# A hybrid attention and SSD layer: V by seven-product jobs, and split operands of x rebuilt on chip at each change of token half

## The chip, the cores and the metric

The kernel runs on one core of a Trainium2 chip. The metric is the device time of one execution in microseconds (us); the time before is the median of three runs. A profile of one further execution is shown beside it. Engines are called by their names in the profile: PE is TensorE (matmuls; PEld its weight loads), DVE is VectorE, ACT is ScalarE, POOL is GpSimd, SP is SyncE, which only issues DMAs. A lower-case q behind an engine's name is its sequencer.

## The reference, cut to what matters

One decoder layer for 2048 tokens of width 1024 in float32. All that the change touches is the input projection `x @ w_in` (1024 x 6672) and, in it, the columns of V and the 16 raw time steps of the SSM.

```python
proj = jnp.einsum('bsd,de->bse', x, w_in[layer])
q, k, v, z_att, z_ssm, xbc, dt_raw = jnp.split(proj, list(SPLITS), axis=-1)
# q, k, v, z_att, z_ssm: 1024 columns each; xbc: 1536; dt_raw: 16
...
o1, l1 = dilated_window_attention(q, k, v, slopes, DILATIONS[0])   # and two more dilations
...
xbc = jax.nn.silu(causal_depthwise_conv(xbc, conv_w[layer], conv_b[layer]))
dt = jax.nn.softplus(dt_raw.astype(jnp.float32) + dt_bias[layer].astype(jnp.float32))
...
y = ssd_chunked(xs_h, dt, a, bm, cm)                                # Mamba-2 scan
...
out = jnp.einsum('bse,ed->bsd', mix, w_out[layer])
x = layer_norm(alpha * x + out, ln_g[layer], ln_b[layer])
```

## The kernel before, in words

**Precision.** A float32 product is made of three fast matmuls. Each operand is split into a high part (ScalarE copies it to the fast type, `nc.scalar.copy`) and a low part (the difference, by VectorE for tokens and by GpSimd for weights), and high x high, low x high and high x low are added up in PSUM.

**The V stage** (lines 90 to 160, driven by the loop over `order` from line 647 on). It comes first. All 1040 columns of V and the time steps are made in plain products with the tokens as stationary operand: for two token halves, three pieces of 348, 346 and 346 columns, eight slices of the contraction and eight groups of 128 tokens, three matmuls each (`v_mm`, L151; 1152 in all). Beside it the stage loads x, splits it (`conv_x`, L140 and L141) and makes and stores what the later jobs need: the split operands of the second token half go to a DRAM tensor `d_T` (`keep_second`), those of the first stay on chip (`T0`) and are stored too (`keep_T`). It also splits half of `w_out`.

**The seven-product jobs.** The other 6144 columns are made 256 columns x 1024 tokens at a time, as a 2 x 2 block product with seven instead of eight block products (Winograd's form of Strassen's method). The token operands of the seven are, in order, `LEFT = ("B11", "T1", "B21", "T2", "B22", "T4", "T3")` with T1 = B12 - B11, T2 = B22 - T1, T3 = B22 - B12, T4 = T2 - B21; each is [128, 4, 512] and has a high and a low part, 16 KB a partition together. The weight operands are A11, S1 = A21 + A22, A12, and so on, made by `column_side` (L288 the sums on VectorE, L295 the high part on ScalarE, L296 the low part on GpSimd). `products` issues 12 matmuls of 512 columns for each of the seven (L340, L342, L344), copies the partial results p1, p5, u2 and p4 out of PSUM on ScalarE (`keep`, L349) into a pool of six buffers `ev`, adds the others to them on VectorE (`put`, L357), and hands each finished block to a `fin`, which stores it a step later. After each product `flush()` runs what was put down for that step with `after(n, f)`; so a job has seven steps, and the side work of the next job (weights, loads) is put down step by step by hand. PE, DVE, ACT and POOL execute in the order in which the program is written (`manual_schedule`); SP's queue is ordered by the scheduler.

**Phases.** Ten jobs work on the first token half, then 22 on the second (their changed weight operands are stored in `d_wc` for reuse), then 12 on the first half again with the weights read back (`column_reload`). At each of the two changes `token_side` reads all seven split operands of the other half, 14 MB, from `d_T` through GpSimd's DMA queue, each as soon as the last job has used the old one. During jobs 1 to 4 the differences T1 to T4 of the second half are made and stored (`sums_load`, `sums_part`, L199 to L203). The time-step arithmetic of the SSM (`decays`, L484 to L520) is spread over steps 12 to 33, and the SSD units (`ssd1` to `ssd5`) run between the products from step 164 on. `copy_v` makes a second copy of V in DRAM in another order of tokens.

**After the projections** come attention for eight pairs of heads (L895 to L978) and the output product with the norm (L1131 to L1169), which the change doesn't touch; attention loads V from `d_v` (L834, L836).

Of the kernel before, what the change touches and what calls it, by code (L numbers as in the profile page):

```python
# [28 lines left out]
def hybrid_layer(ctx, tc, xT, xc, w52, wv, convw, convb, dtb, alog, dskp, gcol, wout,  # L29
# [12 lines left out]
    def dtile(name, shape):  # L42
# [10 lines left out]
    d_T = {(p, n): dtile(f"d_T{p}{n}", [2, 128, 4, 512]) for p in range(2)  # L53
           for n in ("B11", "B21", "B22", "T1", "T2", "T3", "T4")}
# [15 lines left out]
    def evac(i, o, a):  # L70
        if i % 2:
            nc.vector.tensor_copy(o, a)
        else:
            nc.scalar.copy(o, a)

    LEFT = ("B11", "T1", "B21", "T2", "B22", "T4", "T3")
    with ExitStack() as c1:
        pp = c1.enter_context(tc.tile_pool(name="pp", bufs=5, space=PSUM))
        ss = c1.enter_context(tc.tile_pool(name="ss", bufs=3, space=PSUM))

        tp = c1.enter_context(tc.tile_pool(name="tp", bufs=1, reuse_waits="tile"))

        def operand(nm):
            return [tp.tile([128, 4, 512], F32R, name=f"T{nm}{x}") for x in "hl"]  # L90

        def keep_T(nm, a):
            nc.scalar.dma_start(d_T[0, nm][a].rearrange("p k t -> p (k t)"),
                              T0[nm][a].bitcast(F32).rearrange("p k t -> p (k t)"))

        vstage, early = ExitStack(), ExitStack()
        ts = early.enter_context(tc.tile_pool(name="ts", bufs=1, reuse_waits="tile"))
        vp = vstage.enter_context(tc.tile_pool(name="vp", bufs=1, side="right", reuse_waits="tile"))
        T0 = {nm: operand(nm) for nm in ("B11", "B21", "B22")}
        B12 = [vp.tile([128, 4, 512], F32R, name=f"B12{x}") for x in "hl"]  # L100
        second = [operand(f"T{c}") for c in range(1, 5)]

        def x_op(k, i, a):

            if i:
                return second[k // 2][a][:, 2 * (k % 2):2 * (k % 2) + 2]
            left, right = (T0["B11"], B12) if k < 4 else (T0["B21"], T0["B22"])
            return left[a][:, k % 4], right[a][:, k % 4]

        COLS = ((0, 348), (348, 346), (694, 346))  # L110
        vw, vr, rows = {}, {}, {}

        def ask_v(pc, k, queue=nc.gpsimd):
            c0, w = COLS[pc]
            vr[k] = vp.tile([128, 348], F32, name="vraw", bufs=3)[:, 0:w]
            queue.dma_start(vr[k], wv[:, k, c0:c0 + w])
# [1279 lines left out]
```

## Time and profile before

| | |
|---|---|
| median of three runs | 2073.09 us (2069.44 to 2076.03) |
| the profiled execution | 2074.26 us, of it span 2072.5 us |
| PE busy | 1979.0 us, 95% of the span |
| DVE, ACT, POOL busy | 60%, 54%, 52% |
| DMA moved | 481.51 MB, mean 232 GB/s |
| first matmul of the V stage | 6.16 us after the span's start |
| V stage, first to last matmul | 6.16 to 192.7 us |
| seven-product jobs | 192.7 to 1196.9 us |
| attention and output | from there to the end |

A busy PE row counts the pipelined length of each matmul, so the distance between the starts of two matmuls says more than the mean length of one. In the waits, the arrow names what ended an engine's idle time. A row of stretches has one window of time, and in brackets the instructions that lie in it or reach into it.

### The profile page before, as it was taken

What the parts mean: (1) busy time and instruction counts of PE and PEld (TensorE: products, weight loads), DVE (VectorE), ACT (ScalarE), POOL (GpSimd) and SP (SyncE); (2) the same over time, 40 slices, a digit from 0 to 9 for tenths busy, and PEclk for the clock granted to TensorE, in tenths of its full rate; (3) what the DMA queues carried; (4) which work ended last, traced back from release to release, by engine and by line L of the source; (5) the groups of instructions that cost most, each with busy time, mean ns of one, the idle gap of its engine ahead of it and who ended that gap; (6) DMA issues with size and microseconds to landing.
All of it is one profiled execution on the core that took longest, in us unless ns stands there. A gap on an engine that the chain in (4) does not pass through costs nothing.

```text
span 2072.5 us, 42407 instructions
## 1 busy us (share of the span) xinstructions
PE 1979.0 (95%) x15744; PEld 1616.2 (78%) x15744; DVE 1236.8 (60%) x3166; ACT 1125.8 (54%) x3097; POOL 1079.0 (52%) x966
## 2 busy tenths in 40 slices
PE   8999899889999999979999999999899988999998
PEld 8999778778888888858888867667666766888886
DVE  2353666357886656624444368777777846565553
ACT  3433455346655666536566478888778852232221
POOL 4445346656665666735555423687666572422222
PEclk9999999999999999989999999999999999999999
DMA  9797897967678887897878755787877799232210
GB/s 313 268 307 236 267 318 277 368 226 223 202 231 292 276 259 252 321 362 230 275 245 254 250 203 155 223 242 220 239 223 219 230 271 321 96 114 98 89 69 31
DMA packets 238238, 481.51 MB, mean 232 GB/s; under 512 B 38448, under 2 KB 110896, under 8 KB 225872
## 3 DMA queue, kind: packets, MB, share of 16 engines
q1 hardware_dynamic: 147648, 199.52, 30.7%
q0 software_dynamic: 45024, 181.49, 25.9%
q10 hardware_dynamic: 45360, 97.80, 14.9%
q8 instruction: 124, 2.03, 0.4%
q14 instruction: 82, 0.67, 0.1%
HBM read 323.15 MB, written 163.97 MB: 235 GB/s over the span
## 4 chain that ended last, share of the span: by engine, by line
PE 77%; DMA 10%; DVE 5%; ACT 3%; issue 3%; POOL 1%; SPq 1%; ACTq 0%; POOLq 0%; DVEq 0%
PE pp L340 11%; PE pp L344 11%; PE pp L342 11%; PE pp L151 6%; PE N L948 5%; PE S L895 4%; PE S L1131 4%; PE S L1133 3%; PE S L1132 3%; PE ss L151 3%; PE T L922 3%; ACT P L907 2%; PE T L1131 2%; PE T L1132 2%; PE T L1133 2%
## 5 line engine op out<-in xcount | busy, mean ns | idle before, releaser
L296 POOL TENSOR_TENSOR w<-wr,w 128x512 fp32r<-128x512 f32 x231 | 306.1, 1335 | 223.1 <-ACT w L295 173.8
L907 ACT ACTIVATE P<-P,st 128x192 f32<-128x192 f32 (+1 forms) x768 | 322.7, 423 | 72.3 <-DVE st L901 67.4
L901 DVE CUSTOM_DVE_ANT_0 P<-S,tb 128x192 f32<-128x192 f32 (+1 forms) x768 | 206.6, 325 | 98.5 <-PE S L895 80.8
L349 ACT COPY ev<-pp 128x512 f32<-128x512 f32 x176 | 103.0, 585 | 251.7 <-PE pp L344 236.9
L357 DVE TENSOR_TENSOR ev<-pp,ev 128x512 f32<-128x512 f32 x152 | 101.1, 686 | 138.6 <-PE pp L344 95.0
L295 ACT CAST w<-wr 128x512 fp32r<-128x512 f32 x231 | 140.1, 620 | 56.2 <-DVE wr L288 40.0
L1039 POOL TENSOR_TENSOR wb<-num,wb 128x2048 f32<-128x2048 f32 x21 | 95.6, 4551 | 117.4 <-DMA wb<-d_wd 55.1
L907 ACT ACTIVATION_READ_ACCUMULATOR P<-P,st 128x1 f32 x768 | 145.6, 190 | 0.0
L288 DVE TENSOR_TENSOR wr<-wr 128x512 f32<-128x512 f32 x132 | 122.1, 925 | 30.9 <-DMA wr<-w 26.9
L948 PE MATMUL N<-PT,v 128*64 128x64 f32 (+1 forms) x1536 | 126.1, 261 | 12.6 <-ACT num L972 9.0
L924 DVE COPY PT<-T 128x512 f32<-128x512 f32 x192 | 131.8, 686 | 4.6 <-PE T L922 4.6
L922 PE MATMUL T<-ident,P 128*128 128x128 f32 x768 | 129.5, 292 | 1.3 <-DVE st L901 0.9
L922 PEld LDWEIGHTS T<-ident,P 128*128 128x128 f32 x768 | 82.7, 143 | 48.6 <-issue 24.3
L948 PEld LDWEIGHTS N<-PT,v 128*64 128x64 f32 x1536 | 78.8, 138 | 50.6 <-issue 18.9
L895 PE MATMUL S<-k,ex 64*64 64x192 f32 (+1 forms) x2048 | 111.7, 329 | 5.2 <-issue 5.2
L441 DVE SCALAR_TENSOR_TENSOR ss<-U,cw,ss 128x512 f32<-128x512 f32 x144 | 106.0, 751 | 3.7 <-ACT ss L437 1.4
L122 POOL TENSOR_TENSOR vl<-vraw,vh 128x346 fp32r<-128x346 f32 (+1 forms) x48 | 49.1, 1023 | 91.0 <-ACT vh L121 90.8
L1169 POOL TENSOR_TENSOR k<-k,wb 128x1024 f32<-128x1024 f32 x8 | 25.8, 3226 | 121.9 <-DVE k L1168 121.9
L1107 DVE TENSOR_REDUCE tb<-P 128x128 f32<-128x1024 f32 x30 | 60.0, 1999 | 44.9 <-ACT P L1104 22.6
L895 PEld LDWEIGHTS S<-k,ex 64*64 64x64 f32 x2048 | 67.5, 137 | 18.0 <-issue 11.8
L574 DVE TENSOR_TENSOR mt<-mt,ss 128x1024 f32<-128x1024 f32 x32 | 39.0, 1220 | 69.4 <-ACT mt L570 69.0
L565 ACT ACTIVATE mt<-csb,cs 128x128 f32<-128x128 f32 x256 | 78.7, 395 | 3.2 <-DMA csb<-d_cs 2.3
(542 smaller groups left out, 6074.6 us busy)
## 6 DMA issues: line engine op xcount, KB each, us to landing
wr<-w ACTq DMA_DIRECT2D x157, 256.0 KB
wb<-d_wd SPq DMA_DIRECT2D x48, 512.0 KB
d_wc<-w SPq DMA_DIRECT2D x44, 512.0 KB
w<-d_wc POOLq DMA_DIRECT2D x44, 512.0 KB, 6.2
csb<-d_cs ACTq DMA_DIRECT2D x32, 512.0 KB
v<-d_v POOLq DMA_DIRECT2D x16, 1024.0 KB, 6.8
vs<-d_v POOLq DMA_DIRECT2D x16, 960.0 KB, 8.6
st<-xT POOLq DMA_DIRECT2D x20, 512.0 KB, 6.2
```

The source lines that it names most:

```text
L151: nc.tensor.matmul(ps, l if j == 2 else h, vw[k][j % 2], start=(k == j == 0), stop=(k == 7 and j == 2))
L295: nc.scalar.copy(t[:, 0], q[nm])
L296: nc.gpsimd.tensor_tensor(t[:, 1], q[nm], t[:, 0].bitcast(F32), op=OP.subtract)
L340: nc.tensor.matmul(ps, w[:, 0, k], th[:, k], start=start and k == 0, stop=False, skip_group_check=not start)
L342: nc.tensor.matmul(ps, w[:, 0, k], tl[:, k], start=False, stop=False, skip_group_check=not start)
L344: nc.tensor.matmul(ps, w[:, 1, k], th[:, k], start=False, stop=(k == 3), skip_group_check=not start)
L895: nc.tensor.matmul(o, A["q"][d][64 * h:64 * h + 64, blk, 64 * a:64 * a + 64], kv, start=True, stop=True)
L901: nc.vector.tensor_tensor_reduce(P[:, h, cs], sp[h][:, cs], t, -0.125, 3.0e38, OP.add, OP.min, accum_out=stat(A, 0, d, h, blk))
L907: nc.scalar.activation(p, p, AF.Exp, bias=stat(A, 0, d, h, blk), scale=-1.0, accum_out=stat(A, 1, d, h, blk))
L922: nc.tensor.transpose(tp[:, h, i], P[:, h, 256 * i:256 * i + 128], ident)
L924: nc.vector.tensor_copy(pt, tp)
L948: nc.tensor.matmul(o, l, r, start=start, stop=True, skip_group_check=True)
```

## The change

V becomes four wide seven-product jobs of 512 columns x 1024 tokens: V's first half of columns opens phase 0 and phase 1, its second half is the second job of phase 1 and the first of phase 2. In a wide job the tokens are the stationary operand (128 x 128) and 256 weight columns stream; each of the seven products is 16 x 3 matmuls into two PSUM banks (`wide_products`). The weight operands of a wide job are made on chip at its first use, stored (`d_wv`, 1 MB an operand) and read back at its second (`wide_reload`).

The separate V stage, `d_T` and everything that filled it are gone. At the start and at each change of token half, a class `Tokens` loads the four raw blocks of x (1 MB each, `xb`) into places that the old operands have left, and makes the seven split operands from them on VectorE and ScalarE (`STEPS`), put down at steps 3 to 11 counted from the start of the last job of the old half.

The 16 time-step columns leave V's pieces: `steps_of` makes them for each token half during a wide job, with the weights as stationary operand (32 columns: high and low side by side, then 16) and 512 tokens streaming, 32 matmuls a half, and turns the result by twelve small transposes. All 32 half rows of `w_out` are split in steps 8 to 60 (before: half of it in the V stage). `decays` moves into the third wide job. `copy_v` copies V by halves of columns, the second half in phase 2. The pool of weight operands `wp` holds pairs of narrow operands in the tiles of wide ones. There are now 48 jobs (0 to 47) of seven steps; 0, 11, 12 and 35 are the wide ones.

```diff
-        def v_mm(ps, pc, i, r, k, which=(0, 1, 2)):
...
-        def token_side(p):
-
-            T = []
-
-            def step(nm):
-                def f():
-                    T.append([tp.tile([128, 4, 512], F32R, name=f"T{nm}{x}") for x in "hl"])
-                    for a, t in enumerate(T[-1]):
-                        nc.gpsimd.dma_start(t.rearrange("p k t -> p (k t)"),
-                                            d_T[p, nm][a].rearrange("p k t -> p (k t)"))
-                return f
-            return T, [step(nm) for nm in LEFT]
...
+        class Tokens:
...
+            def load(self, n, queue, cuts=1):
+                src = xb[self.p, (0, 1, 3, 2)[n]]
+                if n == 0:
+                    self.r["X"] = x = [wp.tile([128, 512], F32, name="wr", bufs=7) for _ in range(4)]
+                    for k in range(4):
+                        queue.dma_start(x[k], src[:, 512 * k:512 * k + 512])
+                    return
+                nm, at, y = (("R12", "B21", "l"), ("R22", "T4", "l"), ("R21", "T4", "h"))[n - 1]
+                t = self.r[nm] = home(at, y, F32)
...
+            def split(self, nm, src, ks):
+                if ks[0] == 0:
+                    T[nm] = [home(nm, x) for x in "hl"]
+                for s in self.cut(ks, (src,)):
+                    h, l, r = T[nm][0][:, s], T[nm][1][:, s], self.at(src, s)
...
+                    nc.scalar.copy(h, r)
+                    nc.vector.tensor_tensor(l, r, h.bitcast(F32), op=OP.subtract)
...
+            STEPS = (("split", "B11", "X"), ("minus", "X", "R12", "X"), ("split", "T1", "X"),
+                     ("minus", "T2", "R22", "X", ("B22", "l")), ("minus", "X", "R22", "R12"), ("split", "B21", "R21"),
+                     ("minus", "T4", "T2", "R21", ("T3", "l")), ("split", "T2", "T2"), ("split", "B22", "R22"),
+                     ("split", "T4", "T4"), ("split", "T3", "X"))
...
+        def wide_reload(W, s):
+
+            def step(i):
+                nc.gpsimd.dma_start(W[i].rearrange("p a k c -> p (a k c)"), d_wv[s, i])
+            return [lambda i=i: step(i) for i in range(7)]
...
+        def wide_products(W, fin, ramp=False):
+
+            def mm(ps, i, start=True):
+                w, (th, tl) = W[i], T[LEFT[i]]
+                order = [(r, k) for r in range(4) for k in range(4)]
+                if ramp and i < 4:
+                    order.sort(key=lambda x: x[1])
+                for r, k in order:
+                    o, t = ps[r // 2][:, 256 * (r % 2):256 * (r % 2) + 256], slice(r * NJ, r * NJ + NJ)
+                    for j in range(3):
+                        nc.tensor.matmul(o, (th, tl)[j == 1][:, k, t], w[:, int(j == 2), k],
+                                         start=start and r % 2 == k == j == 0, stop=(k == 3 and j == 2),
+                                         skip_group_check=True)
...
+            both = lambda ps: [keep(x) for x in ps]
+            t = [pp.tile([128, 512], F32, name="pp") for _ in range(4)]
+            pa, pc = t[0::2], t[1::2]
+            mm(pa, 0)
+            p1 = both(pa)
+            flush()
+            mm(pc, 1)
+            p5 = both(pc)
+            flush()
+            pb = [ss.tile([128, 512], F32, name="ss") for _ in range(2)]
+            mm(pb, 2)
+            put(0, 0, pb, p1)
+            flush()
+            mm(pa, 3, False)
+            u2 = both(pa)
+            flush()
+            mm(pc, 4, False)
+            put(0, 1, pc, u2)
+            flush()
+            pd = [ss.tile([128, 512], F32, name="ss") for _ in range(2)]
+            mm(pd, 5)
+            p4 = both(pd)
+            flush()
+            mm(pa, 6, False)
+            put(1, 1, pa, p5)
+            put(1, 0, pa, p4, OP.subtract)
+            flush()
...
+            def sums():
+                for pair in (("B11", "B21"), ("T1", "B22")):
+                    ps = ss.tile([128, 512], F32, name="ss")
+                    for a, nm in enumerate(pair):
+                        for k in range(4):
+                            for j, w in ((0, 32), (1, 16)):
+                                nc.tensor.matmul(ps[0:w, :], wd[:, k + 4 * a, 0:w], T[nm][j][:, k],
+                                                 start=(a == k == j == 0), stop=(k == 3 and j == 1), skip_group_check=True)
+                        if a or nm == "B11":
+                            e = ev.tile([128, 512], F32, name="ev")
+                            nc.scalar.copy(e[0:32], ps[0:32])
+                            got.append(e)
...
-        jobs = [(0, x) for x in one_ + conv[4:]]
+        jobs = [(0, ("v", 0))] + [(0, x) for x in one_ + conv[4:]]
+        jobs += [(1, ("v", 0)), (1, ("v", 1))]
         jobs += [(1, x) for x in one_ + [conv[4], rest[0], conv[5]] + rest[1:]]
-        jobs += [(2, x) for x in rest]
+        jobs += [(2, ("v", 1))] + [(2, x) for x in rest]
...
-        spots = [7 * 23 + 3 + 60 * i // 13 if i < 13 else 7 * 32 + 4 * (i - 13) for i in range(32)]
+        spots = [7 * 26 + 2 + 4 * i if i < 13 else 7 * 36 + 4 * (i - 13) for i in range(32)]
...
+                    fs, times = wide_reload(W, i), (1, 3, 6, 7, 8, 9, 10)
...
+            for j in range(32):
+                later.setdefault(8 + 27 * j // 16, []).append(lambda j=j: wout_load(wo, j))
...
+                    if jobs[m + 1][0] != ph:
+                        tok = Tokens(jobs[m + 1][0] % 2)
+                        for t, n in zip((0, 3, 5, 5), range(4)):
+                            after(t, lambda n=n, k=tok: k.load(n, nc.gpsimd))
+                        for t, n in ((3, 0), (5, 1), (6, 2), (6, 3), (6, 4), (7, 5), (7, 6), (8, 7), (9, 8), (10, 9), (11, 10)):
+                            after(t, lambda n=n, k=tok: k.step(n))
```

In the start's own schedule (not shown) SP asks for the weights A11, the x block B11, R12, A21, A22, R22, A12 and R21 in this order. In a wide job `dt` (the three parts of `steps_of`) is put down at steps 3, 5 and 6 of job 0 and 1, 5 and 6 of job 11, and the parts of `decays` at steps 1 to 6 of job 12.

More of the change, by code (lines that the diff above doesn't have):

```diff
@@ L52, in hybrid_layer @@
     d_zs = [dtile(f"d_zs{g}", [16, 128, 2, 4, 64]) for g in range(2)]
[L53 to L54 removed]
+    d_wv = dtile("d_wv", [2, 7, 128, 2048])
     d_cu = [dtile(f"d_cu{i}", [128, 2, 512]) for i in range(12)]
@@ L98, in hybrid_layer @@
[L98 to L116, printed above, removed]
-        def conv_v(pc, k):
-            w, raw = COLS[pc][1], vr[k]
-            vw[k] = vh, vl = [vp.tile([128, 348], F32R, name=f"v{p}{k}")[:, 0:w] for p in "hl"]
-            nc.scalar.copy(vh, raw)
-            nc.gpsimd.tensor_tensor(vl, raw, vh.bitcast(F32), op=OP.subtract)
@@ new lines, in column_load, with load, first @@
+        def column_load(q, ct0, ct1, queue, part=False):
+            def load(nm, ct, h):
+                q[nm] = wp.tile([128, 4, 128], F32, name="wr", bufs=7)
+                queue.dma_start(q[nm], w52[ct][:, 4 * h:4 * h + 4, :])
+            def first():
+                if not part:
+                    q["S1"] = wp.tile([128, 4, 128], F32, name="wr", bufs=7)
+                load("A11", ct0, 0)
+            steps = [first, lambda: load("A12", ct0, 1), lambda: load("A22", ct1, 1)]
+            return steps if part else steps + [lambda: load("A21", ct1, 0)]
@@ new lines, in prepare @@
+        def prepare(m):
+            ph, (kind, i) = jobs[m + 1]
+            wide_now = jobs[m][1][0] == "v"
+            W, q = layout[m + 1], Q.setdefault(m + 1, {})
+            if kind == "v":
+                if ph == 1 and i == 1:
+                    two, fs = column_side(W, q, keep_wide(1))
+                    times = (4, 4, 5, 6, 6, 7, 8, 9, 10)
+                else:
+                    fs, times = wide_reload(W, i), (1, 3, 6, 7, 8, 9, 10)
+            elif ph == 2:
+                fs = column_reload(W, rest.index((kind, i)), q)
+                times = (4, 4, 5, 5, 6, 6, 7) if wide_now else (1, 2, 3, 4, 5, 7, 8)
+            else:
+                u = rest.index((kind, i)) if ph == 1 and (kind, i) in rest else None
+                two, fs = column_side(W, q, keep_sums(u))
+                times = (4, 6, 6, 6, 6, 7, 7, 8, 9) if wide_now else (1, 2 + (m == 1), 3 + (m == 1), 3, 4, 5, 6, 7, 8)
+            for t, f in zip(times, fs):
+                after(t, f)
@@ L777, in hybrid_layer @@
[L777 to L787 removed]
+                    prepare(m)
```

561 lines of the change are left out of this document (258 added, 303 removed).

## The prediction

> **What bounds the kernel now.** I read the page first, then the chain of waits, then busy time by stretches cut at the first matmul of jobs, then the waits of TensorE.
>
> ```profile
> span 2072.5 us, 42407 instructions
> PE 1979.0 (95%) x15744; PEld 1616.2 (78%) x15744; DVE 1236.8 (60%) x3166; ACT 1125.8 (54%) x3097; POOL 1079.0 (52%) x966
> ...
> PE 77%; DMA 10%; DVE 5%; ACT 3%; issue 3%; POOL 1%; SPq 1%; ACTq 0%; POOLq 0%; DVEq 0%
> ```
>
> TensorE is busy nearly always and carries 77% of the chain, so a change pays only through the matmuls' pace or through the holes between them. The stretches say where the holes are (columns: stretch, its length, then per engine the busy time with the count of instructions, last the granted clock, the DMA share and GB/s).
>
> ```profile
> core 0: us, PE busy (x) PEld busy (x) DVE busy (x) ACT busy (x) POOL busy (x), PEclk, DMA share, GB/s
> 6.16:192.70 186.54, 186.54 (x1152) 186.36 (x1153) 75.95 (x100) 71.81 (x134) 99.41 (x134) 1.00 0.87 294
> 230.80:282.10 51.30, 42.88 (x173) 34.28 (x173) 42.00 (x61) 26.11 (x44) 18.57 (x14) 0.93 0.86 298
> 377.80:396.90 19.10, 19.10 (x86) 15.80 (x85) 5.79 (x8) 6.48 (x12) 15.45 (x19) 1.00 0.98 354
> 396.90:432.40 35.50, 24.48 (x85) 17.57 (x84) 5.61 (x10) 6.22 (x12) 14.40 (x17) 0.90 0.98 378
> 879.40:923.80 44.40, 32.39 (x126) 24.57 (x126) 12.84 (x22) 18.75 (x39) 18.77 (x20) 0.81 1.05 392
> 923.80:1196.90 273.10, 273.10 (x1524) 227.33 (x1522) 122.84 (x234) 155.82 (x318) 144.88 (x149) 1.00 0.78 252
> ```
>
> Row 1 is the old V stage, 1152 matmuls without a hole. Row 3 is one undisturbed seven-product job: 84 matmuls (the count takes in two that reach over the edges) in 19.1 us, 0.227 us each at 512 columns. Rows 4 and 5 are the two jobs after a change of token half: the same 84 matmuls take 35.5 us, and 44.4 us where the eleven jobs behind, with the same SSD work among them, take 273.1 / 11 = 24.8 us. Row 2 is two jobs that should take 38.1 us. The waits say what for:
>
> ```profile
> PE pp L340 <- ACT ev L349: 9.3, 4, 5.3
> PE pp L342 <- DMA TB21l<-d_T1B: 3.3, 1, 3.3
> PE pp L342 <- DMA TB21l<-d_T0B: 3.2, 1, 3.2
> ```
>
> At the changes TensorE waits for the split operands that come back from DRAM (14 MB for one half), at 378 to 392 GB/s with the DMA engines full. In row 2 it waits for an eviction by ScalarE, which stands behind the sums of the second half and the time-step chain on VectorE.
>
> **What goes.** The time to the first matmul (6.2, row quoted below), the V stage (186.5), the excess of the two disturbed jobs (51.3 - 38.1 = 13.2), of the first change (35.5 - 19.1 = 16.4) and of the second (44.4 - 24.8 = 19.6): 241.9 us.
>
> **What comes: the V matmuls.** Four wide jobs of 7 products x 16 x 3 = 336 matmuls with 256 columns are 1344, against 1152 with 346. No 256-column matmul of this kind is in the trace; its neighbours are the old V stage, the 512-column rows and the SSD's 128x128 f32 matmuls:
>
> ```profile
> 120.00:150.00 30.00, 30.00 (x190) 30.00 (x190) 1.00 0.91 310
> ...
> L151 PEld LDWEIGHTS pp<-vh,TB11h x48: 187/189/193, 100.8 to 174.8; 128*128 128x128 f32 x48
> ...
> L596 PEld LDWEIGHTS ss<-bc,H x240: 187/192/333, 711.8 to 1173.6; 128*128 128x128 f32 x120
> L596 PE MATMUL ss<-bc,H x240: 272/275/422, 712.0 to 1173.7; 128*128 128x128 f32 x120
> ...
> 711.98 1.05 PE L596 MATMUL ss<-bc,H 128*128 128x128 f32 x8
> ```
>
> In the V stage's 30 us 190 matmuls are counted, about 1.5 of them cut off by the edges: 0.159 us each. From 0.159 at 346.7 columns and 0.227 at 512 the slope is 0.41 ns a column, and 256 columns come to 0.159 - 90.7 x 0.00041 = 0.122 us. From below the SSD row bounds it: eight matmuls with a new weight each take 1.05 us from the first start to the last end, the last alone 0.275, so (1.05 - 0.275) / 7 = 0.111 us, with weight loads as long (192 ns) as those of V (189 ns). From above the V stage's own 0.159 bounds it: there the weight loads fill the row without a gap (PEld 30.00 of 30), so the loads and not the columns could be what sets it. I take 0.122: it lies on the line of two rows of the same type, and the SSD row shows that loads of that length can follow one another faster. 1344 x 0.122 = 164.0 us (149.2 to 213.7).
>
> **The time steps.** 64 matmuls of 512 columns at 0.227 are 14.5 us, all on TensorE's path. In each half the first partial sum is copied out (ScalarE) before the bank is added to: about 1.0 us a half, 2.0 together. Then the transposes, which stand in TensorE's queue ahead of the next job, need three eviction buffers. The wide job holds two each for its p5 and p4 at that point, of six; two come from the stored u2, the third must wait until p5 is added to and stored, behind product 6. The rows of the costliest groups, one of an old operand split, and the landing of the DMAs on V's tensor give the prices:
>
> ```profile
> L296 POOL TENSOR_TENSOR w<-wr,w 128x512 fp32r<-128x512 f32 x231 | 306.1, 1335 | 223.1 <-ACT w L295 173.8
> ...
> L349 ACT COPY ev<-pp 128x512 f32<-128x512 f32 x176 | 103.0, 585 | 251.7 <-PE pp L344 236.9
> L357 DVE TENSOR_TENSOR ev<-pp,ev 128x512 f32<-128x512 f32 x152 | 101.1, 686 | 138.6 <-PE pp L344 95.0
> L295 ACT CAST w<-wr 128x512 fp32r<-128x512 f32 x231 | 140.1, 620 | 56.2 <-DVE wr L288 40.0
> ...
> L288 DVE TENSOR_TENSOR wr<-wr 128x512 f32<-128x512 f32 x132 | 122.1, 925 | 30.9 <-DMA wr<-w 26.9
> ...
> L141 DVE TENSOR_TENSOR TB11l<-st,TB11h x4: 693/694/1005, 48.7 to 71.3; 128x512 fp32r<-128x512 f32 x4
> ...
> DMA to landing us min/median/max: 3.2/6.7/14.7
> ```
>
> An add (0.7), a store at the shortest landing (3.2), a copy (0.6) and 12 short transposes (about 1): 5.5 us a half (1 if the buffer is free early, 9 at the median landing), 11.0. Together 27.5 us (18.5 to 34.5).
>
> **The start.** The first product needs 0.75 MB of raw weights and x where the old one needed 0.43.
>
> ```profile
> 6.16 1.92 PE L151 MATMUL pp<-vh,TT1h 128*128 128x348 f32 x5 [6.16 <-ACT TT1h L140]
> ...
> 0.00:6.00 6.00, 0.00 (x0) 0.00 (x0) 0.00 (x0) 2.27 (x3) 1.26 (x7) 1.00 0.64 149
> 6.00:8.00 2.00, 1.84 (x6) 1.66 (x7) 1.29 (x2) 1.21 (x3) 0.04 (x1) 1.00 0.91 258
> 8.00:14.00 6.00, 6.00 (x29) 6.00 (x28) 2.97 (x4) 3.92 (x5) 4.13 (x5) 1.00 1.04 400
> ```
>
> At 149 and 258 GB/s that is 0.6 us more: first matmul at 6.8. Product 0 (48 x 0.122 = 5.9, and about 2 for slow first matmuls: 29 in the 6 us from 8 on, 0.207 each) ends near 14.7. Product 1 needs R12, the end of the first 2.5 MB: 0.9 MB by 6 us, 1.4 by 8, 2.5 at 10.8. From there VectorE makes T1 (four differences and four low parts of 512 at 0.69: 5.5), then the weight sum of 1024 (1.3); ScalarE casts it (1.2), GpSimd takes its low part (2 x 1.335 = 2.7): 21.5. That is a wait of 7 us. Product 3 waits another 2 in the same way (its weights are the last of the sums). With the slow first matmuls: 11 us (5 to 16).
> L288's mean of 0.925 beside L141's 0.694 shows VectorE held up by something while GpSimd splits weights. The Trainium skill (SBUF — State Buffer, "SBUF: two separate sides") says that a GpSimd instruction and a VectorE one with two SBUF inputs exclude each other for their whole length. By it one GpSimd split of 2.7 us would stand inside the chain above and the predicted time would be about 2.7 us higher; the two rows agree with it in direction.
>
> **The changes of token half.** Instead of 14 MB, 4 MB of raw x and 7 MB of wide weights are asked for, over the 19 us of the last job and the 41 of the wide one. VectorE rebuilds: 24 operations of 512 and 10 of 1024, 24 x 0.69 + 10 x 1.3 = 29.6 us, from step 3 of the last job (11 us before its end) to product 6 of the wide one (35 us after): it fits if the raw blocks come in time. R22 and R21 can only be asked for when product 5 of the last job frees T4; 2 MB at 400 GB/s are 5 us and the landing 3.2, so VectorE may stand still for some 5 us, and product 2 (11.8 us after the boundary) wants B21 as the 22nd of the 34. I put 3 us for each change, 6 in all (0 to 16, the latter if every operation takes L288's 0.925). Behind VectorE's wait stand only its own later rebuilding steps: the adds of the last job's product 6 are queued ahead of them.
>
> **Small terms.** The decay chain moves into the third wide job, and its matrix product stands in TensorE's queue behind product 5, while VectorE starts on it after product 2, 17.7 us before: its seven pairs and the rest, about 14 us, leave 3 us to wait.
>
> ```profile
> L496 DVE TENSOR_TENSOR h<-h,z x7: 419/426/1391, 243.0 to 264.2; 128x256 f32<-128x256 f32 x7
> L497 DVE TENSOR_SCALAR h<-h x7: 293/294/1426, 243.4 to 265.5; 128x256 f32<-128x256 f32 x7
> ```
>
> At the end of the first and third wide job the next one's weight sum is queued behind four adds (4 x 0.69) on VectorE, then 0.7 + 0.62 + 1.34 for the sum and its split, against one product of 2.7 that covers it: 3 us after the third, 1 beyond the transposes after the first. At the end of the projections V's tiles may lie on T4's and be loaded some 5 us later than now; three steps of scores cover most of it: 1 us. Sum 3 + 3 + 1 + 1 = 8.
> At nothing I cost the 32 splits of w_out spread over steps 8 to 60 (before, half of them ran at 0.75 a step, now all at 0.6), the 32 column-half copies of V, which queue on GpSimd among loads asked for a job ahead, the d_wv stores on SP (14 MB for the 28 MB of split x that go), and the SSD units now every 4 steps, as they already were in the last row of the stretches. If SP's stores came late, the ev buffers would be late: that is a rival.
>
> **The sum.** 6.8 + 164.0 + 27.5 + 11 + 6 + 8 = 223.3 comes, 241.9 goes: 18.6 us less. The profiled execution took 2074.3 us (span 2072.5), 1.2 above the median of 2073.1. 2074.3 - 18.6 - 1.2 = 2054.5 us.
>
> **Rivals.** (a) *The pace is the SSD row's.* At 0.111 the wide jobs take 149.2 and the time is 2040. For it: the loads there are as long. Against: that row is plain f32 at two passes, and both rows of V's own type carry about 15 ns over their columns.
> The Trainium skill (TensorE: Matmul & The Clock Gate, "Back-to-back issue gap") gives N/2.4 + 2.5 ns, 109 ns for 256 columns, and with it about 2037; the 512-column row, 227 ns against its 216, does not agree.
> (b) *The six eviction buffers.* A wide product takes two, and p4 needs those of p1, whose stores are asked for after product 3 and must have landed when product 5 ends, 11.8 us later, with megabytes of d_wv on the same queue. With the slowest landing of the row above, 14.7, each wide job waits 2.9 there, and with the median, 6.7, the transposes 3.5 more a half: 4 x 2.9 + 2 x 3.5 = 18.6, and the time is 2073, no change.
> (c) *The weight load is the floor.* If a 128-column load cannot follow the last one in under 0.159, as the gapless PEld row of V allows, the wide jobs take 213.7 and the time is 2104: slower. It decides from 0.122 + 18.6 / 1344 = 0.136 us a matmul. Against it stands only the SSD row.
>
> **Chances.** Forecast 0.55 (its own range 2042 to 2066), (a) 0.20, (b) 0.12, (c) 0.13. From these: faster by over 0.3% (about 6 us, what a measurement of this kernel can tell from no change) 0.75, within it 0.12, slower 0.13. The range leaves out (c) and the far ends: 2033 to 2078.
>
> **What would show it.** Starts of the V matmuls 0.122 us apart; the first near 7 us and a hole near 15 to 21; 8 us of time-step matmuls behind product 5 in two wide jobs and a hole of 5 behind product 6; no wait of TensorE for a split operand from DRAM, and holes under 5 us at the changes. Wrong, if V's matmuls lie 0.136 or more apart, or if holes inside the wide jobs add up to over 40 us.

## The result and the profile after

The changed kernel takes 2054.55 us (median of four runs, 2053.84 to 2055.98); beside it the kernel before took 2071.94 (four runs, 2069.44 to 2076.03). The ratio is 0.9915, 95% interval 0.9897 to 0.9933: faster by 17.4 us. The forecast was 2054.5 us: 18.6 us off the profiled execution of before, and another 1.2 for that execution's distance from the median.

The page of the changed kernel, its lines that answer to those of before:

```profile
span 2052.1 us, 42770 instructions
...
PE 1967.2 (96%) x16024; PEld 1602.3 (78%) x16024; DVE 1274.4 (62%) x3197; ACT 1128.8 (55%) x3079; POOL 1042.5 (51%) x885
...
DMA packets 231791, 447.73 MB, mean 218 GB/s; under 512 B 39488, under 2 KB 113728, under 8 KB 220576
...
PE 82%; ACT 4%; DMA 4%; DVE 3%; issue 3%; POOL 1%; SPq 0%; ACTq 0%; POOLq 0%; DVEq 0%
```

280 more matmuls, 11.8 us less TensorE time, 34 MB less through the DMA engines, and DMA's part of the chain down from 10% to 4%: the waits for split operands from DRAM are gone. The stretches of the changed kernel, cut at the first matmul of jobs (columns as in the prediction):

```profile
core 0: us, PE busy (x) PEld busy (x) DVE busy (x) ACT busy (x) POOL busy (x), PEclk, DMA share, GB/s
7.74:71.87 64.13, 55.23 (x381) 49.72 (x381) 47.80 (x47) 27.18 (x38) 19.08 (x7) 0.92 0.57 222
93.95:112.99 19.04, 19.04 (x85) 15.77 (x84) 9.94 (x13) 10.66 (x18) 12.63 (x13) 1.00 0.78 259
265.31:322.39 57.08, 52.08 (x382) 46.98 (x380) 34.23 (x43) 21.11 (x31) 7.46 (x7) 0.94 0.70 261
322.39:365.53 43.14, 41.64 (x344) 41.36 (x343) 22.21 (x37) 12.88 (x21) 14.34 (x7) 1.00 0.56 198
365.53:386.15 20.62, 19.76 (x87) 15.71 (x86) 14.31 (x16) 7.74 (x14) 16.77 (x16) 1.00 0.43 130
832.11:878.79 46.68, 43.46 (x337) 43.06 (x336) 29.23 (x37) 19.06 (x28) 7.25 (x10) 0.93 0.79 279
326.00:338.00 12.00, 12.00 (x103) 12.00 (x102) 2.53 (x4) 3.85 (x6) 4.85 (x3) 1.00 0.71 231
```

Rows 1, 3, 4 and 6 are the wide jobs 0, 11, 12 and 35, rows 2 and 5 the narrow jobs 2 and 13. The last row is 12 us inside job 12 without a hole: 103 matmuls are counted, some two of which reach over the edges, and their starts lie 0.120 us apart (the median over the wide jobs). So a wide job without a hole would take 336 x 0.120 = 40.3 us, and what a row has beyond that is holes, slow clock and time steps. The waits of TensorE say what for (line waited for: us in total, times, longest; most of the lines left out belong to attention):

```profile
...
PE pp L301 <- ACT TB11h L132: 7.7, 1, 7.7
PE pp L301 <- DVE TT1l L133: 5.1, 2, 2.6
...
PE ss L301 <- DVE TB21l L133: 3.6, 1, 3.6
...
PE pp L301 <- ACT w L209: 2.1, 1, 2.1
PE pp L301 <- ACT TT1h L132: 1.9, 2, 1.3
...
PE pp L301 <- POOL w L210: 1.9, 1, 1.9
...
PE ss L523 <- issue: 1.5, 1, 1.5
```

The first is the time to the first matmul, 7.74 us. Two stages are left that wait: the start (TB21l, and the weights w from ScalarE and GpSimd), and product 1 of the wide jobs behind the changes, which waits at each for T1 (TT1h, TT1l).

### The profile page after: what moved, and what is told of

It is laid out like the page before. It is cut to its first block, busy times and chain, and to the rows that moved or that the text cites. A ratio compares the mean times of both kernels' runs of the same rounds, so it can differ in the third digit from the quotient of the medians.

```text
span 2052.1 us, 42770 instructions
## 1 busy us (share of the span) xinstructions
PE 1967.2 (96%) x16024; PEld 1602.3 (78%) x16024; DVE 1274.4 (62%) x3197; ACT 1128.8 (55%) x3079; POOL 1042.5 (51%) x885
## 4 chain that ended last, share of the span: by engine, by line
PE 82%; ACT 4%; DMA 4%; DVE 3%; issue 3%; POOL 1%; SPq 0%; ACTq 0%; POOLq 0%; DVEq 0%
PE pp L252 13%; PE pp L256 13%; PE pp L254 13%; PE N L977 6%; PE S L924 4%; PE pp L301 4%; PE S L1160 4%; PE S L1162 3%; PE S L1161 3%; PE T L951 3%; ACT P L936 3%; PE ss L301 2%; PE T L1160 2%; PE T L1161 2%; PE T L1162 2%
## 5 line engine op out<-in xcount | busy, mean ns | idle before, releaser
L210 POOL TENSOR_TENSOR w<-wr,w 128x512 fp32r<-128x512 f32 x224 | 296.2, 1333 | 226.5 <-ACT w L209 175.9
L244 ACT COPY ev<-pp 128x512 f32<-128x512 f32 x200 | 116.9, 586 | 333.6 <-PE pp L256 271.2
L209 ACT CAST w<-wr 128x512 fp32r<-128x512 f32 x224 | 133.7, 619 | 35.2 <-DVE wr L202 19.6
L202 DVE TENSOR_TENSOR wr<-wr 128x512 f32<-128x512 f32 x128 | 111.1, 868 | 15.6 <-DMA wr<-w 9.0
L252 PE MATMUL pp<-TT1h,w 128*128 128x512 f32 x176 | 69.8, 397 | 1.9 <-ACT w L209 1.9
```

The source lines that it names most:

```text
L209: nc.scalar.copy(h, r)
L210: nc.gpsimd.tensor_tensor(l, r, h.bitcast(F32), op=OP.subtract)
L252: nc.tensor.matmul(ps, w[:, 0, k], th[:, k], start=start and k == 0, stop=False, skip_group_check=not start)
```

## The experiments

**What the transfers of before cost.** The kernel before without `token_side`'s loads at the two changes:

```diff
-                    if ph2 != ph:
-                        nT, steps = token_side(ph2 % 2)
-                        for j in range(7):
-                            after(j, steps[j])
```

> The kernel before with the reading back of the split operands left out at both changes of token half: the jobs go on with the old half's operands, so the second half's projections are not computed. Theory (the two changes cost the kernel before 36 us, because TensorE waits for 14 MB from DRAM): ratio to before 0.983, about 2036 us, and the two jobs behind the changes take 19.1 and about 24.5 us. Rival (the waits only show a stretch in which something else would have held TensorE): under 15 us less, 2057 us or more.

2035.98 us (2034.43 to 2041.47), ratio 0.9828 (0.9801 to 0.9855): as expected. In the stretch that held one job of 35.5 us there now lies no hole:

```profile
396.90:432.40 35.50, 35.50 (x158) 29.42 (x157) 23.93 (x30) 15.35 (x27) 21.28 (x22) 1.00 0.32 101
```

The job behind the second change takes 23.53 us instead of 44.37. This is the first source of the gain, shown by taking it away: the two changes were worth 36 us of waiting for 28 MB.

**What the rebuilding costs instead.** The changed kernel without `Tokens` at the changes:

```diff
-                    if jobs[m + 1][0] != ph:
+                    if False:
```

> The changed kernel with the loading of raw x and the rebuilding left out at both changes, so that the second half's projections are not computed. Theory (what is left of the changes is the late landing of R12 and the slow clock behind it, 7 us and 6.4 us): the wide jobs behind the changes take 50.2 and 40.4 us, total about 2041 us, ratio 0.985. Rival (the reading back of the wide weights holds them): the wide jobs stay at 57 and 46.7, 2054 us.

2041.17 us (2038.77 to 2043.18), ratio 0.9847 (0.9818 to 0.9876). Jobs 11 and 35 without the rebuilding:

```profile
269.23:319.33 50.10, 48.96 (x381) 44.36 (x379) 10.88 (x13) 9.12 (x15) 8.04 (x7) 1.00 0.67 236
829.02:869.33 40.31, 40.31 (x337) 40.31 (x336) 4.75 (x7) 6.99 (x12) 6.79 (x10) 1.00 0.77 239
```

Job 35 is then 336 matmuls of 0.120 and nothing else, job 11 the same with 9.8 us of time steps. From first matmul to first matmul jobs 11 and 35 of the changed kernel take 57.07 and 46.69 us. So the rebuilding, its loads of x included, costs 57.07 - 50.10 = 7.0 us at the first change and 46.69 - 40.31 = 6.4 at the second: 13.4 instead of the 36 for the loads of before.

**Which block comes late.** In the changed kernel R12 (the block TB21l<-xb) is asked for at step 3 of the last job, and VectorE, which makes T1 from it, stands at it. VectorE's wait at the first change, GpSimd's issue of the load, and stretches around it:

```profile
DVE wr L123 <- DMA TB21l<-xb: 9.5, 1, 9.5
```

```profile
258.14 0.55 POOL L111 DMA_DIRECT2D TB21l<-xb  x1
```

```profile
250.00:254.00 4.00, 4.00 (x20) 3.30 (x19) 0.00 (x0) 1.46 (x3) 3.57 (x6) 1.00 0.17 57
...
266.00:270.00 4.00, 4.00 (x36) 4.00 (x35) 0.00 (x0) 0.00 (x0) 0.52 (x1) 1.00 1.03 427
270.00:274.00 4.00, 1.61 (x12) 1.21 (x10) 2.88 (x5) 2.15 (x4) 0.53 (x1) 1.00 1.03 426
274.00:278.00 4.00, 2.53 (x12) 2.53 (x13) 4.00 (x8) 3.23 (x5) 0.00 (x0) 0.53 1.04 413
```

Issued at 258.14, the block is there at 271.1, 13 us later: the DMA engines are nearly empty in the 4 us from 250 (57 GB/s) and full in the last 5 us of its way (rows from 266 and 270: 427 and 426). TensorE then has its hole (1.61 of 4 us busy), and the slow clock comes behind it (0.53 in the last row). The edit asks for R12 one step earlier and also splits T1 one step earlier, ahead of two adds on VectorE:

```diff
-                        for t, n in zip((0, 3, 5, 5), range(4)):
+                        for t, n in zip((0, 2, 5, 5), range(4)):
...
-                        for t, n in ((3, 0), (5, 1), (6, 2), (6, 3), (6, 4), (7, 5), ...
+                        for t, n in ((3, 0), (5, 1), (5, 2), (6, 3), (6, 4), (7, 5), ...
```

> The changed kernel with R12 asked for at step 2 in place of 3 (ahead of the second wide weight operand on GpSimd's queue) and T1 split at step 5 in place of 6. Theory (the hole at the changes is R12 landing 13 us after it was asked for, behind 3 MB on full DMA engines): no wait for T1 at either change, no slow clock behind it, 12 us less than the changed kernel, 2042 us, ratio 0.986. Rival (the engines are full whatever the order, another block is then late): under 4 us less, 2050 us or more.

2047.58 us (2046.28 to 2048.38), ratio 0.9879 (0.9856 to 0.9902): 7 us less in the medians, where 12 were expected. The wait for T1 is gone at both changes, and jobs 11 and 35 take 54.33 and 44.56 us, 4.9 us less together; the other 2 lie behind the projections, which the edit doesn't touch. VectorE starts on R12 3.9 us earlier (267.27 instead of 271.12), and 1.2 us more come from the order of T1 and the adds. What is late next at the first change are the split of B21 and a block of weights, at the second a block of weights alone:

```profile
PE ss L301 <- DVE TB21l L133: 1.4, 2, 1.3
...
PE ss L301 <- DMA w<-d_wv: 0.6, 1, 0.6
```

```profile
PE ss L301 <- DMA w<-d_wv: 2.5, 1, 2.5
```

So both hold in part: R12, and with it T1, was late first, and with that gone other megabytes on the same engines are late.

**What bounds the pace of V's matmuls.** Each wide matmul cut into two of 128 columns, each with its own weight load:

```diff
-                        nc.tensor.matmul(o, (th, tl)[j == 1][:, k, t], w[:, int(j == 2), k],
+                        for c in range(2):
+                            s = slice(128 * c, 128 * c + 128)
+                            nc.tensor.matmul(o[:, s], (th, tl)[j == 1][:, k, t], w[:, int(j == 2), k, s],
```

> The changed kernel with every wide matmul cut into two of 128 columns, each with its own weight load: 2688 instead of 1344. If a matmul costs its columns and about 13 ns (128 / 2.4 + 13.5 = 67 ns), the wide jobs take 180 us in place of 161.3: 2073 us. If the weight load is a floor at the 111 ns of the SSD's 128-column row, they take 298: 2191 us. I hold the floor for likelier, since it would lie just under the 120 ns measured at 256 columns.

2285.68 us (2232.12 to 2291.28), slower than either expectation. No ratio is formed from it; what is used are distances between matmuls inside the profiled execution. They have two values. These are 20 us each of jobs 0, 11 and 12:

```profile
20.00:40.00 20.00, 20.00 (x96) 20.00 (x95) 16.09 (x14) 4.01 (x5) 6.04 (x3) 1.00 0.60 236
...
350.00:370.00 20.00, 20.00 (x181) 20.00 (x181) 14.81 (x20) 7.98 (x11) 1.06 (x2) 1.00 0.64 238
440.00:460.00 20.00, 20.00 (x96) 20.00 (x96) 0.00 (x0) 2.12 (x3) 2.36 (x1) 0.50 0.17 67
```

181 in 20 us at the full clock are 0.111 us each, at half the columns: the floor of a matmul with a new 128-column weight, the same that the prediction read from the SSD row. There it could have come from the columns (an f32 record of 512 columns takes 0.435 us in a run below, a quarter of that is 0.109). Here it can't: at the 0.41 ns a column of the prediction's line, 128 columns would come to 0.07. Jobs 11 and 35 keep the floor: job 35 takes 74.99 us, and 672 x 0.111 are 74.6. At 256 columns the 0.120 lie just above it, so rival (c), a floor at 0.159, is excluded, and rival (a) was its floor and not its pace. In job 12 the clock is granted at half and the distance is 0.213. Job 0 has the same 0.213 up to 132.8 us. Its row shows a clock of 1.00, but the clock record of this execution begins only at 132.8, and the weight loads take 333 ns in jobs 0 and 12 against 192 in job 11. That is why the run is slower than the 2191 us of the floor: jobs 0 and 12 take 143.9 and 145.1 us.

**The start: two engines that stop each other.** VectorE in the changed kernel while it makes the first operands, and GpSimd beside it (start, length, then line, operation and count):

```profile
16.66 1.22 DVE L202 TENSOR_TENSOR A<-A,A 128x1024 f32<-128x1024 f32 x1
17.98 3.23 DVE L202 TENSOR_TENSOR A<-S,A 128x1024 f32<-128x1024 f32 x1
21.14 6.86 DVE L123 TENSOR_TENSOR TB22l<-TT4l,wr 128x512 f32<-128x512 f32 x4
27.92 2.48 DVE L123 TENSOR_TENSOR wr<-TT4l,TB21l 128x512 f32<-128x512 f32 x4
```

```profile
17.78 2.35 POOL L210 TENSOR_TENSOR w<-S,w 128x1024 fp32r<-128x1024 f32 x1 [11.18 <-ACT w L209]
20.09 3.36 POOL L210 TENSOR_TENSOR w<-w,w 128x1024 fp32r<-128x1024 f32 x1
24.17 2.67 POOL L210 TENSOR_TENSOR w<-A,w 128x1024 fp32r<-128x1024 f32 x1 [0.72 <-ACT w L209]
```

A sum of 1.22 takes 3.23 and four differences of 2.48 take 6.86 exactly where GpSimd's splits lie: 6.4 us of VectorE. The edit gives these splits to VectorE itself:

```diff
-                    nc.gpsimd.tensor_tensor(l, r, h.bitcast(F32), op=OP.subtract)
+                    (nc.vector if i in fast else nc.gpsimd).tensor_tensor(l, r, h.bitcast(F32), op=OP.subtract)
...
-            two, wsteps = column_side(layout[0], Q[0], keep_wide(0))
+            two, wsteps = column_side(layout[0], Q[0], keep_wide(0), (1, 2, 3))
```

> The changed kernel, but in its first wide job the low parts of the weight operands 1, 2 and 3 are made on VectorE instead of GpSimd. Nothing is left out. Theory: the two engines hold each other up there (VectorE's four differences took 6.86 us at the spot and 2.5 us elsewhere, one sum 3.23 us and 1.22 us elsewhere, while GpSimd's 1024-wide low parts ran); then the wait for TB21l (3.6 us) and that for GpSimd's low part (1.9 us) shrink together to about 0.5 us: 5 us less than the changed kernel, some 2049.5 us, ratio to the kernel before about 0.989. Rival: VectorE alone is the bound of the start, and three more operations on it only lengthen its queue: no less time than the changed kernel (0.9915), or some us more.

2046.03 us (2044.61 to 2047.54), ratio 0.9875 (0.9840 to 0.9911). VectorE after the edit:

```profile
18.82 1.22 DVE L210 TENSOR_TENSOR w<-S,w 128x1024 fp32r<-128x1024 f32 x1
19.96 1.22 DVE L202 TENSOR_TENSOR A<-S,A 128x1024 f32<-128x1024 f32 x1
21.09 1.22 DVE L210 TENSOR_TENSOR w<-w,w 128x1024 fp32r<-128x1024 f32 x1
22.23 2.49 DVE L123 TENSOR_TENSOR TB22l<-TT4l,wr 128x512 f32<-128x512 f32 x4
24.64 2.49 DVE L123 TENSOR_TENSOR wr<-TT4l,TB21l 128x512 f32<-128x512 f32 x4
```

The same operations at their quiet length, two splits among them, and the last of them ends at 27.1 instead of 30.4 though this execution began 1.2 us later. By these rows the rival, VectorE as the bound, is out. That the two exclude each other is what the prediction took from the Trainium skill (SBUF — State Buffer, "SBUF: two separate sides"); these rows agree with it. TensorE's waits shrink less than expected: TB21l from 3.6 to 2.5, and 0.8 and 0.7 for others in place of GpSimd's 1.9. Job 0 is 3.6 us shorter in the profile (60.54), but it began 1.2 us later and job 1 is 1.8 longer. Counted to the first matmul of job 2, which is what the edit can reach, this kernel needs 93.43 us, and the four kernels here with the start as it was need 93.95, 94.34, 96.88 and 97.87. So the edit is worth some 2 us there (0.5 to 4.4), which these profiles don't tell apart from scatter. The rest of the 9 us between the spans lies in job 11, where no slow clock came behind the hole this time, in job 35 and behind the projections, none of which the edit touches.

**The time steps by column groups.** The core of the edit; the transposes and the sums over the groups become eight small matmuls with a matrix of zeros and ones:

```diff
-                            for j, w in ((0, 32), (1, 16)):
-                                nc.tensor.matmul(ps[0:w, :], wd[:, k + 4 * a, 0:w], T[nm][j][:, k],
...
+                        for j in range(2):
+                            for k in range(4):
+                                nc.tensor.matmul(ps[32 * k:32 * k + 32, :], wd[:, k + 4 * a].bitcast(F32), T[nm][j][:, k].bitcast(F32),
```

> The changed kernel, but its time steps are made by plain f32 matmuls with 32-column weights, in four column groups of the array (PSUM partitions 0, 32, 64, 96), ten per group and half; the sums over the groups and the transposes together are eight small matmuls with a matrix of zeros and ones. Nothing is left out. Now a half costs 8.2 us of matmuls and 1.6 us behind product 6, 9.8 us. Theory: matmuls in different column groups run side by side, so ten of 0.43 us are 4.3 us, the eight small ones 0.9, one handover 0.7: about 6 us a half, 8 us less in all, some 2046.5 us, ratio about 0.988. Rival: they run one after the other: 40 x 0.43 = 17 us a half, 15 us more in all, some 2070 us, ratio about 0.999.

2049.13 us (2042.85 to 2053.04), ratio 0.9887 (0.9847 to 0.9928): not told apart from the changed kernel's 0.9915. The time steps themselves, and the small matmuls:

```profile
56.50:65.20 8.70, 8.70 (x81) 2.50 (x80) 0.00 (x0) 1.17 (x2) 0.00 (x0) 1.00 0.17 62
71.10:72.80 1.70, 1.70 (x18) 1.70 (x17) 1.49 (x3) 0.00 (x0) 0.00 (x0) 1.00 0.17 58
```

Neither the theory nor the rival came true. In the trace four matmuls of the four groups start within 20 ns (at 56.530, 56.536, 56.543, 56.550), the next four at 56.98: they do run side by side. But each f32 matmul is two records of 0.43 us, and the expectation had counted 0.43 for both: 40 matmuls are 80 records, in fours 20 x 0.435 = 8.7 us, against 8.2 now. And the small ones cost two records of 0.11 each, though they have 16 columns: 1.7 us, against 1.6 now. What did change is job 1: 19.17 us instead of 22.09, of which more below.

**The order of two queues.** The next job's loads ahead of the time steps' copies in job 0, and the weight sum behind a wide job at step 5:

```diff
-                times = (4, 6, 6, 6, 6, 7, 7, 8, 9) if wide_now else ...
+                times = (4, 5, 5, 6, 6, 7, 7, 8, 9) if wide_now else ...
...
+                if m == 0:
+                    ask(m, 1, nc.scalar)
+                    ask(m, 2, nc.scalar)
                 if m + 1 < len(jobs):
                     prepare(m)
```

> The changed kernel, but in job 0 the next job's loads stand on ScalarE's queue ahead of the time steps' copies, and the weight sum of the narrow job behind a wide one is made at step 5 rather than 6. Nothing is left out. Theory: the waits at the start of jobs 1 (3.05 us over a quiet job) and 13 (1.58 us) come from the order on the queues alone and go: about 4 us less than the changed kernel, some 2050.5 us, ratio about 0.9895. Rival: the wait passes to the next one of the queue (GpSimd's low part of the weight): no change, 0.9915.

2054.57 us (2052.39 to 2063.99), ratio 0.9929 (0.9906 to 0.9951): no change, as the rival had it, but not by its mechanism. Jobs 1 and 13 take 19.21 and 19.15 us, their waits are gone. Job 0 has a new one, in the time steps. TensorE's first matmul behind it, and ScalarE's queue:

```profile
63.91 0.42 PE L362 MATMUL ss<-TB21h,wdr 128*32 128x512 f32 x1 [4.54 <-ACT ev L366]
```

```profile
57.58 0.85 ACTq L157 DMA_DIRECT2D wr<-w  x2
62.77 0.62 ACT L209 CAST w<-wr 128x512 fp32r<-128x512 f32 x1 [4.61 <-DVE wr L202]
63.29 0.57 ACT L366 COPY ev<-ss 32x512 f32<-32x512 f32 x1
```

The cast of job 1's weights now stands ahead of the copy that TensorE needs, and itself waits for the loads that were just asked for. In job 12 the earlier sum stands ahead of the decays on VectorE: the wait for L523 grows from 1.5 to 3.1 us, job 12 from 43.15 to 46.29. On queues in program order the wait goes to whoever stands second.

**Four edits at once, then the changed kernel again and two combinations.** The four are the edits of R12, of the splits in the start, of the column groups and of the order:

> The changed kernel with four edits at once: R12 loaded one step earlier and T1 split one step earlier (measured by itself at 7 us less), the low parts of the start on VectorE, the time steps in four column groups, and the order of the queues at jobs 1 and 13. Nothing is left out. If each is worth what its theory says and they don't overlap: 7 + 5 + 8 + 4 = 24 us less than the changed kernel, some 2030 us, ratio about 0.980. Rival: the first and the third free TensorE only to wait sooner for the same loads and sums: 10 us or less, 2044 us and up, ratio 0.987 or more.

2040.89 us (2036.56 to 2047.22), ratio 0.9848 (0.9799 to 0.9897): between the two, and 14 us less than the changed kernel's ratio gives (0.0067 x 2069). Jobs 12 and 13 together take 65.4 us, against 63.8 in the changed kernel: the order edit costs more there than it brings.

> The changed kernel itself once more, unaltered, beside the two that follow, for its scatter from run to run: ratio 0.9915 as before if that scatter is within its interval. In the profile the waits for T1 behind both changes (1.3 and 2.6 us) should stand there again to 0.1 us, since they come from the order of the transfers; the half clock behind them, 6.8 us twice in the first profile and missing at job 11 in that of another kernel with the same wait, is expected to vary, and with it job 11 between 53 and 57 us.

2054.63 us (six runs, 2048.11 to 2060.43), ratio 0.9924 (0.9906 to 0.9941). The waits for T1l are 2.6 us at both changes again, those for T1h 1.7 and 0.4 where they were 1.3 and 0.6; the half clock behind job 11's hole lasts 6.8 us again, that behind job 35's 3.4 instead of 6.8. Jobs 0 and 1 took 66.15 and 24.57 us (64.13 and 22.09 in the first profile), so a profile of the start is good to some 4 us.

> The changed kernel with two edits: R12 loaded one step earlier with T1 split one step earlier, and the low parts of the start on VectorE. Nothing is left out. Each by itself gave about 7 us; they lie in different stages (the jobs behind the changes, and job 0). Theory: both are waits that TensorE really stood at, so their gains add: 12 to 14 us less than the changed kernel, ratio to the kernel before about 0.985. Rival: most of the 7 us of the edit in the start was scatter (its profile shows 3.6 us less in job 0 and 3.9 us less in jobs that it doesn't touch): 9 to 10 us less, ratio about 0.987.

2041.76 us (2038.78 to 2048.57), ratio 0.9873 (0.9855 to 0.9891), 0.0051 or 10.5 us less than the changed kernel on the same chip by the ratios, 12.9 by the medians. Each ratio is known to some 4 us, so this doesn't decide between the theory (12 to 14) and the rival (9 to 10). The profiles say more of the two edits: in the four kernels that ask for R12 earlier, jobs 11 and 35 together take 96.1 to 99.4 us, and in the five profiles with the rebuilding as it was and 256 columns 99.1 to 103.8, so that edit is worth some 4 us in the mean; the first matmul of job 2 comes at 93.22 us, as with the splits alone.

> The kernel of the run before with the time steps in four column groups too, and the order of the queues as in the changed kernel. Nothing is left out. In the profile of that edit by itself the time steps took as long as now, but the wait at the start of job 1 (3.05 us) was gone, as one copy fewer stands ahead of the loads. Theory: that wait is TensorE's alone, so 2 to 3 us less than the run before, ratio about 0.984; jobs 12 and 13 together 63.8 us, as in the changed kernel, and not 65.4 as with the four edits. Rival: the wait passes to the weights of job 1 on GpSimd, no difference.

2036.17 us (2034.00 to 2038.38), ratio 0.9836 (0.9824 to 0.9848): 5.6 us less than the run before in the medians, 3.8 in the spans, and the fastest version that computes everything. Jobs 0 and 1 of it:

```profile
6.40:69.26 62.86, 57.11 (x432) 49.53 (x433) 45.85 (x51) 26.53 (x37) 12.33 (x5) 0.95 0.62 241
69.26:88.43 19.17, 19.17 (x86) 15.87 (x86) 10.75 (x13) 9.96 (x18) 12.78 (x10) 1.00 0.58 196
```

Job 0 is 1.8 us longer than in the run before (61.09), job 1 5.3 shorter (24.46): with two copies instead of three the loads of job 1 are issued on ScalarE's queue at 61.85, right behind the second copy. In the changed kernel they are issued at 70.90, just behind the start of the third copy. Jobs 12 and 13 take 63.7 together. So the wait that the order edit only moved goes away when the copy in front of it is not needed.

## Why the prediction was right, point by point

What went was read from rows of before and went. What came, term by term, in the first profile of the changed kernel:

| term | predicted | measured | from |
|---|---|---|---|
| first matmul | 6.8 | 7.7 | start of job 0 (6.2 in a second profile) |
| 1344 wide matmuls | 164.0 | 161.3 | 0.120 each, not 0.122 |
| time steps | 27.5 | 19.6 | 2 x (8.2 + 1.6) |
| waits in the start | 11 | 14.0 | 64.13 - 40.3 - 9.8 |
| the two changes | 6 | 13.4 | 57.07 - 40.3 - 9.8 and 46.69 - 40.3 |
| small terms | 8 | 7.5 | 43.15 - 40.3, 20.62 - 19.04, 22.09 - 19.04 |
| sum | 223.3 | 223.5 | |

That the sum agrees to 0.2 us is luck: 11.1 us too much in three terms (matmuls, time steps, small terms) cancel 11.3 too little in the others. The terms don't hold everything either. 241.9 - 223.5 is 18.4 us, but up to the last matmul of the projections the changed kernel is 21.5 us shorter (1175.3 instead of 1196.8), and behind it 1.1 longer (876.8 instead of 875.6), within the scatter of that part (869 to 876 in the profiles of the other kernels with the change). Of the 3.1 us that no term holds 1.2 belong to the second change: the prediction read its cost as 19.6 from the mean of the eleven jobs behind, and without the loads that job took 20.8 less. The rest, some 2 us, is spread over the narrow jobs, and its cause stays open.

**The pace** was right: 0.120 against 0.122. The line through the 346- and 512-column rows holds, and the 128-column run shows the floor under it at 0.111. The gapless weight-load row of before, on which rival (c) stood, was no floor. The Trainium skill's figure for the gap (TensorE: Matmul & The Clock Gate, "Back-to-back issue gap"), 109 ns for 256 columns, would be 11 ns low here; that section itself says that its formula leaves out the weight load, which each matmul here has.

**The time steps: the step that failed** is the ev buffer. The prediction let the third copy wait for p5 to be added to, copied out and stored behind product 6. In the changed kernel it waits, but not for a store. ScalarE's third copy and TensorE's transposes in job 0:

```profile
70.88 0.57 ACT L366 COPY ev<-ss 32x512 f32<-32x512 f32 x1 [9.28 <-PE ss L373]
```

```profile
70.36 0.68 PE L373 MATMUL ss<-ident,ev 32*128 32x32 f32 x8
71.51 0.43 PE L373 MATMUL ss<-ident,ev 32*128 32x32 f32 x4 [0.47 <-ACT ev L366]
71.87 0.50 PE L252 MATMUL pp<-TB11h,w 128*128 128x512 f32 x1
```

The profile names the transposes as what releases it, and in both halves of seven of the kernels with three copies the third begins 0.52 us after the first transpose, to 2 ns. So the eight transposes of the first two copies run, the third copy begins beside them, and TensorE waits 0.47 us for it. The likely reading is that it takes the buffer of the first copy, free after its four transposes (the fourth ends at 70.79). In the 128-column run, where product 6 lasts longer, the third copy does what the prediction had: it begins ahead of the transposes, released by the landing of a store of V.

```profile
149.05 0.57 ACT L368 COPY ev<-ss 32x512 f32<-32x512 f32 x1 [11.87 <-DMA d_v<-ev]
```

There the copy waits for other semaphores, so the program had given it another buffer. But the step that made the term too large is an overlap. The prediction put the add and the store behind product 6, one after the other. In the changed kernel the first half of product 6 fills one bank, and VectorE adds p5's first half to it while the second half runs:

```profile
67.59 0.69 DVE L307 TENSOR_TENSOR ev<-pp,ev 128x512 f32<-128x512 f32 x1 [12.46 <-PE pp L301]
```

Its store is issued at 68.30. By the landing after 2.7 us, as in the 128-column run, the buffer of the prediction would have been free at about 71.0 (an estimate), hardly later than the third copy began. What the prediction put at 11 us for both halves was about 3 (2 x 1.6). Rival (b) is out: without the rebuilding, job 35 runs its 336 matmuls without any hole (40.31 of 40.31 us busy), so no wide product waited there for an eviction buffer.

**The changes** were sized at 3 us each and measured 7.0 and 6.4, inside the bounds (0 to 16 for both). The mechanism was right, VectorE standing at a raw block that is late, but the block was wrong: not R22 and R21, asked for last, with B21 waiting behind them, but R12, asked for at step 3 into full DMA engines, with T1 behind it. Of the 7.0 us, 3.9 are TensorE's two waits and the rest fits the slow clock behind them. The block that the prediction named does come late once R12 does not: in the fastest version ScalarE stands 3.9 us at its cast of R21 behind the second change, and TensorE waits 2.4 us for an eviction queued behind that cast.

**The start** was sized at 11 and measured 14.0. The hole at product 1 came where it was put (between 15.4 and 20.3 in two pieces, 4.0 us of waiting, less than the 7 forecast); the second came one product earlier than forecast and was 3.6 instead of 2, in part because VectorE lost 6.4 us to GpSimd: without that loss 2.5 were left. The prediction had told of this loss only as an addition of 2.7. The term that was mis-sized is another: waits make up 7.6 us, and the other 6.4 are matmuls at 0.213 us and more instead of 0.120, the first twenty and those behind two of the holes, for which the prediction had put 2.

**The small terms**: 2.9 (decays), 1.6 (the sum behind the third wide job) and 3.1 (job 1) for 3, 3 and 1, and nothing for the handover to attention. Job 1's was the one under-sized, through a copy ahead of the loads on ScalarE's queue.

## What to carry to other kernels

Replacing a transfer by arithmetic on chip pays the difference between two waits, and the second one is set by the first block that the arithmetic needs: ask for that one before the queue is full, ahead of megabytes that are needed later. A sum that comes out right can hold errors of 10 us in both directions, so compare it term by term before a next change is built on it. On engines that execute in program order, moving an instruction forward hands its wait to the one behind it; taking an instruction out removes it.

## What the runs showed of the hardware

VectorE and GpSimd, each with two operands in SBUF, stop each other: 6.4 us of VectorE lost in the 9 us in which three splits on GpSimd took 8.4. The sum that VectorE began 0.2 us behind the first split ended 1.1 us behind that split's end, about its own quiet length of 1.22.

A stream of matmuls with 128 columns and a new weight each can stay at the half clock although no hole is in it. In the profiled execution of the 128-column run this happened twice: job 12 took 145.1 us at 0.213 us a matmul, with a granted clock of 0.50 from 429.8 to 576.5 and PE busy 20.00 of 20, and job 0 kept the same distance from its start to 132.8. Both times the full clock came 2 to 4 us after the first 512-column matmuls; jobs 11 and 35, the same code, ran at 0.111 throughout. The Trainium skill (TensorE: Matmul & The Clock Gate, "What's actually happening") has the full clock come after about 3.4 us of sustained work. These streams don't agree; in the other runs the slow stretches behind holes last 3.4 or 6.8 us, once or twice that time. What sent the clock down at 429.8, 2.3 us after job 12 had begun at the full clock, was not tried. The fastest of the four executions of this kernel took 53.6 us less than the median; how long its streams were slow is not known.

Four f32 matmuls with 32-column weights in four column groups start within 20 ns and take the time of one, 0.43 us a record; a f32 matmul is two records in the trace, and one of 16 columns still costs 0.11 us for each of them.
